# Modulation vectors in unbroken steps of three weight chunks, with GpSimd's queue for their loads and sums

## The chip, the cores and the metric

The kernel runs on one core of a Trainium2 chip. The metric is the device time of one execution in microseconds (us); lower is better. TensorE (PE) multiplies, VectorE (DVE) and ScalarE (ACT) do elementwise work, GpSimd (POOL) does some of it and issues DMAs, SyncE (SP) issues most DMAs. Each engine works through its own list of instructions in order and waits on semaphores for the others.

## The reference

A first block of two layers (attention beside a long convolution) is followed by a second one (a mixer, a dense feed-forward part, a state-space mixer, a mixture of experts). Each of the four parts of the second block has a modulation, computed from one vector `c`:

```python
def adaln(c, w, b):
    m = jax.nn.silu(c.astype(jnp.float32)) @ w + b
    shift, scale, gate = jnp.split(m, 3, axis=-1)
    return shift[:, None, :], scale[:, None, :], gate[:, None, :]
...
    sh, sc, g = adaln(c, e_mod_mix_w[j], e_mod_mix_b[j])
    h = rmsnorm(x, e_norm_mix[j]) * (1.0 + sc) + sh
```

`c` has 1024 elements and `w` is 1024 x 3072, float32, so each modulation is one row times 12.6 MB of weights: 50.3 MB for the four, each element used once.

## The kernel before

The four modulations don't depend on `x`, so the kernel computes them in the background of the first block. Python generators are registered as tasks with a rate. The projections of the first block call `tick` after each piece of work (some 57 times from the start of the first layer to the point named below), and a tick lets a task take as many steps (`yield` to `yield`) as its rate has added up to: 0.65 per tick for `modulations` (`ADALN_RATE` 65). A scheduler then puts all instructions into an order for each engine, so the order of the program isn't the order on the engine. Ahead of the last projection of the second layer `self.finish(self.adalns)` (L903) takes all steps that are left.

`modulations` waits `ADA_SKIP` = 8 steps and then runs `adaln` for four keys. The weights lie in memory as 24 chunks of 512 KB per modulation (128 partitions x 4 KB), one for each 128 outputs. A group is four chunks. Each chunk is loaded on SyncE's queue into one of three buffers `rawm` (`AR_BUFS`), and eight small matmuls (L947) multiply it: the 1024 inputs stand in eight columns of `silu`, and pairs of them land on four separate groups of 32 partitions of the PSUM tile `acc`, the 32 rows of a group all alike. After every second chunk there is a `yield` (`ADA_STEP` = 2), so that other work can come between. When four chunks are done, ScalarE copies `acc` to `ads` (L952), TensorE transposes it in four pieces (L955), and VectorE adds the four partial sums into `adv` (L956). After six groups come the bias and the norm's gain, one more transpose (L963), and the gate's row goes to memory on SyncE's queue (L966). These are 13 steps per modulation, 60 with the eight skipped.

The projections' weights take the same SyncE queue: `wchunk` loads 512 KB into one of a few `raw` buffers (L264), ScalarE rounds it to `whi` (L207), VectorE subtracts for `wlo` (L210), and three matmuls use them (L220 to L222, L322 to L324 where the weights are the left operand). At the end of a layer `x_done` computes the row statistics of x, TensorE transposes x with them (L439), and the first projection of the next part can begin. A load into a `rawm` buffer waits until the eight matmuls of the chunk that was in it are done, and whatever stands behind it on its queue waits too.

Of the kernel before, what the change touches and what calls it, by code (L numbers as in the profile page):

```python
# [14 lines left out]
AF = mybir.ActivationFunctionType  # L15
ALU = mybir.AluOpType
AX = mybir.AxisListType
# [3 lines left out]
P = 128  # L21
# [97 lines left out]
class Net:  # L119
    def __init__(self, ctx, tc, a, out):  # L120
        self.ctx, self.tc, self.nc, self.a, self.out = ctx, tc, tc.nc, a, out
        self.uid, self.ring, self.extra, self.left, self.hold, self.held = 0, {}, 0, 0, None, 0
        self.tasks = []
        self.dq = (tc.nc.gpsimd, tc.nc.sync, tc.nc.scalar)[DQ]
        self.gate, self.pool_lo = [], 0
        self.rows, self.cols = {}, {}
        e = ctx.enter_context
        self.cst = e(tc.tile_pool(name="cst", bufs=1))
        self.act = e(tc.tile_pool(name="act", bufs=1))
        self.mod = e(tc.tile_pool(name="mod", bufs=1))  # L130
        self.sm = e(tc.tile_pool(name="sm", bufs=8))
        self.ps = e(tc.tile_pool(name="ps", bufs=1, space=PSUM))
        self.dram = e(tc.tile_pool(name="dr", bufs=1, space=DRAM))
        self.wp = e(tc.tile_pool(name="wp", bufs=1, reuse_waits="tile"))
        self.raws, self.hls = [(self.wp, RAW_BUFS)], [(self.wp, HL_BUFS)]
# [770 lines left out]
    def first_block(self):  # L906
        pool = lambda name: self.tc.tile_pool(name=name, bufs=1, reuse_waits="tile")
        with pool("b1") as self.b1:
# [9 lines left out]
            for l in range(2):  # L918
                if l == 0:
                    self.adalns = self.task(self.modulations(), ADALN_RATE / 100)  # L920
                self.first_layer(l, H)
# [1 line left out]
            self.finish()  # L923


    def adaln(self, key, pool, raw_alloc):

        nc, a = self.nc, self.a  # L930
        V = nc.vector
        w = a[key + "_w"]
        cols = self.cols[key] = self.t(self.cst, [P, 2, 8], "col" + key)
        row = self.rows[key] = self.t(self.dram, [D], "row" + key)
        bc = self.load(self.sm, a[key + "_c"], [P, 4, 8], "adb", bufs=1, eng=self.dq)
        ad = self.t(self.sm, [P, 24], "adv", bufs=1)
        silu = self.silu_cols(pool)
        for m0 in range(0, 24, 4):
            acc = self.psB()
            for m in range(m0, m0 + 4):  # L940
                raw = raw_alloc()
                nc.sync.dma_start(raw, w[m])
                cs = slice((m - m0) * P, (m - m0 + 1) * P)
                for r in range(2):
                    for j in range(4):
                        k = 2 * j + r
                        nc.tensor.matmul(acc[32 * j:32 * j + 32, cs], silu[:, k:k + 1].broadcast_to([P, 32]),  # L947
                                         raw[:, k * P:(k + 1) * P], start=r == 0 and m == m0, stop=r == 1, skip_group_check=True)
                if m % ADA_STEP == ADA_STEP - 1 and m < m0 + 3:
                    yield  # L950
            s = self.t(pool, [P, 512], "ads", bufs=1)
            nc.scalar.activation(s, acc, AF.Copy)  # L952
            pt = self.psB()
            for i in range(4):
                nc.tensor.transpose(pt[:, i * P:(i + 1) * P], s[:, i * P:(i + 1) * P], self.ident)  # L955
            V.tensor_reduce(ad[:, m0:m0 + 4], pt.rearrange("p (m j r) -> p m j r", m=4, j=4)[:, :, :, 0], AX.X, ALU.add)  # L956
            yield
        V.tensor_tensor(cols[:, 1], ad[:, 0:8], bc[:, 0], ALU.add)
        V.scalar_tensor_tensor(cols[:, 0], ad[:, 8:16], 1.0, bc[:, 1], ALU.add, ALU.add)
        V.tensor_tensor(cols[:, 0], cols[:, 0], bc[:, 3], ALU.mult)  # L960
        V.tensor_tensor(bc[:, 2], ad[:, 16:24], bc[:, 2], ALU.add)
        pt = self.psB()
        nc.tensor.transpose(pt[0:8, 0:P], bc[:, 2], self.ident)  # L963
        r = self.t(self.act, [P, P], "dg", bufs=2)[0:8, :]
        nc.scalar.copy(r, pt[0:8, 0:P])
        self.dq.dma_start(row.rearrange("(m n) -> m n", n=P), r)  # L966
        yield

    def silu_cols(self, pool):
# [10 lines left out]
    def modulations(self):  # L980
        raw = lambda: self.t(self.b1, [P, D], "rawm", bufs=AR_BUFS)
        for _ in range(ADA_SKIP):
            yield
        for k in ("e_mod_mix", "e_mod_ffn", "o_mod_mix", "o_mod_ffn"):
            yield from self.adaln(k, self.b1, raw)
            if k == "e_mod_ffn":
                for _ in range(ADA_SKIP1):
                    yield

    def adaln_task(self, key, pool, rate):  # L990
        return self.task(self.adaln(key, pool, self.raw), rate)

    def gate_row(self, key):
        self.mgt = self.bcast(self.mod, self.rows[key], D, "mgt")
# [944 lines left out]
LATE1 = 0  # L1939
LATE2 = 0  # L1940
PRIO = 3000
ADALN_RATE = 65
S5_RATE = 70
RAW2_BUFS = 11
RAW3_BUFS = 5
# [98 lines left out]
AR_BUFS = 3  # L2044
# [12 lines left out]
MGV = 3  # L2057
HOLDP = 2
HOLDC = 0
ADA_STEP = 2  # L2060
ADA_SKIP = 8
ADA_SKIP1 = 0
```

## Time and profile before

| | us |
|---|---|
| median of 3 runs | 1993.03 (1983.26 to 1996.6) |
| profiled execution | 1992.76 |
| its span | 1991.0 |
| TensorE busy | 1869.4 (94%) |
| VectorE busy | 1555.7 (78%) |
| ScalarE busy | 1190.1 (60%) |
| GpSimd busy | 196.9 (10%) |

The first block ends near 570 us; the mixer begins near 641 us, the dense part near 800. Matmuls are pipelined and their ends are modelled, so busy time of TensorE is an upper figure. float32 matmuls leave two records each (L947: 768 matmuls, 1536 records).

### The profile page before, as it was taken

The numbers are of one execution on the slowest core, as the hardware profiler recorded it, in microseconds if no ns is written. First come the engines' busy times: TensorE is split into PE (matmuls) and PEld (weight loads), VectorE is DVE, ScalarE is ACT, GpSimd is POOL, SyncE is SP. The second block draws the span as 40 slices with busy tenths as digits, with TensorE's granted clock in tenths as the row PEclk, the third lists the DMA queues.
The fourth block names the chain that finished last, engine by engine and source line by source line (L and its number), as shares of the span: only waits on it lengthen the run. The fifth ranks groups of instructions, "written<-read, shape, count | busy, mean of one in ns | idle before, by whom it ended". The sixth has DMA issues, their size and how long they took to land.

```text
span 1991.0 us, 31217 instructions
## 1 busy us (share of the span) xinstructions
PE 1869.4 (94%) x11450; PEld 1580.4 (79%) x11450; DVE 1555.7 (78%) x2484; ACT 1190.1 (60%) x1628; POOL 196.9 (10%) x319
## 2 busy tenths in 40 slices
PE   7899989999976998889988989999999999999997
PEld 6787767887754977779978978888888888888875
DVE  6687577686432756788878678999999999999897
ACT  6564445554322843434445358787788877877775
POOL 0000000000010011872212210010001000100000
PEclk9999999999977987999999789999999999999999
DMA  8635656755687631557666568999999999999991
GB/s 259 193 121 171 209 177 210 253 161 191 221 280 237 174 102 51 173 210 234 216 238 251 216 238 282 374 323 377 352 369 316 379 353 378 324 382 357 356 346 57
DMA packets 254826, 503.37 MB, mean 253 GB/s; under 512 B 20082, under 2 KB 97396, under 8 KB 252616
## 3 DMA queue, kind: packets, MB, share of 16 engines
q1 hardware_dynamic: 253848, 498.47, 72.5%
q0 software_dynamic: 816, 2.82, 0.4%
q8 instruction: 92, 1.51, 0.3%
q14 instruction: 70, 0.57, 0.1%
HBM read 485.47 MB, written 15.75 MB: 252 GB/s over the span
## 4 chain that ended last, share of the span: by engine, by line
PE 77%; DVE 8%; DMA 6%; issue 3%; POOL 3%; ACT 3%; SPq 0%; ACTq 0%; DVEq 0%; POOLq 0%
PE A L220 12%; PE A L222 12%; PE A L221 12%; PE B L220 6%; PE B L221 6%; PE B L222 6%; PE A L322 3%; PE A L323 3%; PE A L324 3%; PE B L947 3%; DVE wlo L210 2%; DMA k<-in_flt_deltas_dram 1%; DMA rawm<-in_o_mod_ffn_w_dram 1%; PE B L1743 1%; PE B L439 1%
## 5 line engine op out<-in xcount | busy, mean ns | idle before, releaser
L210 DVE TENSOR_TENSOR wlo<-raw,whi 128x1024 fp32r<-128x1024 f32 x777 | 935.0, 1227 | 190.1 <-ACT whi L207 178.7
L207 ACT ACTIVATE whi<-raw 128x1024 fp32r<-128x1024 f32 x777 | 813.5, 1057 | 369.9 <-PE A L222 141.6
L221 PE MATMUL A<-wlo,hTh 128*128 128x512 f32 (+1 forms) x752 | 288.6, 384 | 1.6 <-DVE wlo L210 1.3
L220 PE MATMUL A<-whi,hTh 128*128 128x512 f32 (+1 forms) x752 | 285.4, 387 | 4.2 <-ACT hTh L207 4.2
L222 PE MATMUL A<-whi,hTl 128*128 128x512 f32 (+1 forms) x752 | 286.9, 383 | 0.9 <-DVE hTl L210 0.9
L322 PE MATMUL A<-hTh,whi 128*128 128x256 f32 x864 | 248.4, 288 | 7.7 <-ACT whi L207 4.3
L324 PE MATMUL A<-hTh,wlo 128*128 128x256 f32 x864 | 246.6, 285 | 1.4 <-DVE wlo L210 1.4
L323 PE MATMUL A<-hTl,whi 128*128 128x256 f32 x864 | 246.8, 286 | 1.0 <-DVE hTl L210 1.0
L322 PEld LDWEIGHTS A<-hTh,whi 128*128 128x128 f32 x864 | 167.1, 193 | 12.0 <-ACT whi L207 4.5
L323 PEld LDWEIGHTS A<-hTl,whi 128*128 128x128 f32 x864 | 167.3, 194 | 3.6 <-issue 1.4
L324 PEld LDWEIGHTS A<-hTh,wlo 128*128 128x128 f32 x864 | 167.2, 193 | 3.7 <-DVE wlo L210 1.8
L220 PEld LDWEIGHTS A<-whi,hTh 128*128 128x128 f32 x752 | 141.7, 189 | 35.4 <-ACT hTh L207 4.9
L221 PEld LDWEIGHTS A<-wlo,hTh 128*128 128x128 f32 x752 | 141.8, 189 | 33.3 <-DVE wlo L210 4.9
L222 PEld LDWEIGHTS A<-whi,hTl 128*128 128x128 f32 x752 | 142.0, 189 | 31.0 <-DVE hTl L210 2.0
L221 PE MATMUL A<-wlo,xg 128*128 128x512 f32 (+1 forms) x384 | 143.5, 374 | 0.0
L222 PE MATMUL A<-whi,xg 128*128 128x512 f32 (+1 forms) x384 | 143.0, 372 | 0.0
L220 PE MATMUL A<-whi,xg 128*128 128x512 f32 (+1 forms) x384 | 141.7, 376 | 0.0
L221 PE MATMUL B<-wlo,mhh 128*128 128x512 f32 x352 | 138.7, 394 | 0.0
L222 PE MATMUL B<-whi,mhl 128*128 128x512 f32 x352 | 137.6, 391 | 0.0
L220 PE MATMUL B<-whi,mhh 128*128 128x512 f32 x352 | 120.9, 394 | 0.2 <-ACT mhh L207 0.2
L947 PE MATMUL B<-rawm,silu 128*32 128x128 f32 x1536 | 70.8, 312 | 22.0 <-DMA rawm<-in_o_mod_ffn_w_dram 14.3
L947 PEld LDWEIGHTS B<-rawm,silu 128*32 128x32 f32 x1536 | 45.0, 122 | 47.8 <-DMA rawm<-in_o_mod_ffn_w_dram 20.6
(575 smaller groups left out, 2974.1 us busy)
## 6 DMA issues: line engine op xcount, KB each, us to landing
raw<-in_o_exp_up_dram SPq DMA_DIRECT2D x176, 512.0 KB, 5.8
raw<-in_o_exp_down_dram SPq DMA_DIRECT2D x176, 512.0 KB, 6.1
raw<-in_o_exp_gate_dram SPq DMA_DIRECT2D x174, 512.0 KB, 5.7
raw<-in_w_in_dram SPq DMA_DIRECT2D x96, 512.0 KB, 5.1
rawm<-in_e_mod_mix_w_dram SPq DMA_DIRECT2D x24, 512.0 KB, 3.7
rawm<-in_e_mod_ffn_w_dram SPq DMA_DIRECT2D x24, 512.0 KB, 6.6
rawm<-in_o_mod_mix_w_dram SPq DMA_DIRECT2D x24, 512.0 KB, 4.9
raw<-in_e_w_in_dram SPq DMA_DIRECT2D x24, 512.0 KB, 4.2
```

What stands on the lines that cost most here:

```text
L207: nc.scalar.activation(hi, src, AF.Copy)
L210: (nc.gpsimd if lo_eng == "pool" else nc.vector).tensor_tensor(lo, src, hi.bitcast(F32), ALU.subtract)
L220: nc.tensor.matmul(out, ah, bh, start=first, stop=False)
L221: nc.tensor.matmul(out, ah, bl, start=False, stop=False)
L222: nc.tensor.matmul(out, al, bh, start=False, stop=last)
L322: nc.tensor.matmul(o, wh[:, ms], xh[:, k, :], start=k == 0 and m == 0, stop=False, **kw)
L323: nc.tensor.matmul(o, wh[:, ms], xl[:, k, :], start=False, stop=False, **kw)
L324: nc.tensor.matmul(o, wl[:, ms], xh[:, k, :], start=False, stop=k == 7, **kw)
L439: nc.tensor.matmul(o, x[:, ks], dg, start=True, stop=True)
L947: nc.tensor.matmul(acc[32 * j:32 * j + 32, cs], silu[:, k:k + 1].broadcast_to([P, 32]), raw[:, k * P:(k + 1) * P], start=r == 0 and m == m ...
L1743: nc.tensor.transpose(ptr[:, i * P:(i + 1) * P], sg[:, i * P:(i + 1) * P], self.ident)
```

## The change

Each step of `adaln` now takes three chunks in one piece, with no `yield` inside and under a high priority (`self.first()`), so that the scheduler puts their 24 matmuls behind each other. The loads are issued from GpSimd's queue (`self.mq`), by `fetch`: the first three ahead of a modulation's first step, and those of the next step at the end of a step. Within a step the chunk that was loaded last is multiplied first. ScalarE copies 384 columns. The transposes and sums of each group are replaced: four small DMAs per step, also on GpSimd's queue, take one row of each of the four partition groups (3 x 512 bytes) to the tile `adp` of 96 rows, and at the end of a modulation one transpose of 96 rows and one sum over four give all 24 columns. The bias load and the gate's row use GpSimd's queue as well. A modulation has 10 steps (48 in all with the eight skipped), at a rate of 0.80 per tick. The loads of the projections' weights stay on SyncE's queue.

```diff
-    def adaln(self, key, pool, raw_alloc):
+    def adaln(self, key, pool, raw_alloc, bufs):
...
-        bc = self.load(self.sm, a[key + "_c"], [P, 4, 8], "adb", bufs=1, eng=self.dq)
+        bc = self.load(self.sm, a[key + "_c"], [P, 4, 8], "adb", bufs=1, eng=self.mq)
         ad = self.t(self.sm, [P, 24], "adv", bufs=1)
+        parts = self.t(self.sm, [96, P], "adp", bufs=1)
         silu = self.silu_cols(pool)
-        for m0 in range(0, 24, 4):
+
+        def fetch(m0):
+            raws = [raw_alloc() for _ in range(bufs)]
+            for i in range(bufs):
+                self.mq.dma_start(raws[i], w[m0 + i])
+            return raws
+
+        raws = fetch(0)
+        yield
+        for m0 in range(0, 24, bufs):
             acc = self.psB()
-            for m in range(m0, m0 + 4):
-                raw = raw_alloc()
-                nc.sync.dma_start(raw, w[m])
-                cs = slice((m - m0) * P, (m - m0 + 1) * P)
-                for r in range(2):
-                    for j in range(4):
-                        k = 2 * j + r
-                        nc.tensor.matmul(acc[32 * j:32 * j + 32, cs], silu[:, k:k + 1].broadcast_to([P, 32]),
-                                         raw[:, k * P:(k + 1) * P], start=r == 0 and m == m0, stop=r == 1, skip_group_check=True)
-                if m % ADA_STEP == ADA_STEP - 1 and m < m0 + 3:
-                    yield
-            s = self.t(pool, [P, 512], "ads", bufs=1)
-            nc.scalar.activation(s, acc, AF.Copy)
-            pt = self.psB()
-            for i in range(4):
-                nc.tensor.transpose(pt[:, i * P:(i + 1) * P], s[:, i * P:(i + 1) * P], self.ident)
-            V.tensor_reduce(ad[:, m0:m0 + 4], pt.rearrange("p (m j r) -> p m j r", m=4, j=4)[:, :, :, 0], AX.X, ALU.add)
+            with self.first():
+
+                for i in reversed(range(bufs)):
+                    cs = slice(i * P, (i + 1) * P)
...
+                s = self.t(pool, [P, bufs * P], "ads", bufs=1)
+                nc.scalar.activation(s, acc[:, :bufs * P], AF.Copy)
+            for j in range(4):
+                self.mq.dma_start(parts[24 * j + m0:24 * j + m0 + bufs], s[32 * j:32 * j + 1].rearrange("o (m p) -> o m p", m=bufs))
+            if m0 + bufs < 24:
+                raws = fetch(m0 + bufs)
             yield
+        pt = self.psB()
+        nc.tensor.transpose(pt[:, 0:96], parts, self.ident[0:96, 0:96])
+        V.tensor_reduce(ad, pt[:, 0:96].rearrange("p (j m) -> p m j", j=4), AX.X, ALU.add)
...
-        self.dq.dma_start(row.rearrange("(m n) -> m n", n=P), r)
+        self.mq.dma_start(row.rearrange("(m n) -> m n", n=P), r)
...
-            yield from self.adaln(k, self.b1, raw)
-            if k == "e_mod_ffn":
-                for _ in range(ADA_SKIP1):
-                    yield
+            yield from self.adaln(k, self.b1, raw, AR_BUFS)
...
-ADALN_RATE = 65
+ADALN_RATE = 80
```

On TensorE, at the end of the first block, the list of before holds the last matmuls of the output projection (`A<-whi,hTh`), then the modulations' chunks and transposes up to the transposed x (L439); of its 32 chunks behind the projection the first eight stand here:

```order
L222 MATMUL A_6249<-whi_6282,hTl_5598 128x512
L955 MATMUL B_5747<-ident_78,ads_5745 128x128 x4
L947 MATMUL B_5753<-rawm_5754,silu_1532 32x128 x8
L947 MATMUL B_5753<-rawm_5764,silu_1532 32x128 x8
L947 MATMUL B_5753<-rawm_5774,silu_1532 32x128 x8
L947 MATMUL B_5753<-rawm_5784,silu_1532 32x128 x8
L955 MATMUL B_5796<-ident_78,ads_5794 128x128 x4
L947 MATMUL B_5802<-rawm_5803,silu_1532 32x128 x8
L947 MATMUL B_5802<-rawm_5813,silu_1532 32x128 x8
L947 MATMUL B_5802<-rawm_5823,silu_1532 32x128 x8
L947 MATMUL B_5802<-rawm_5833,silu_1532 32x128 x8
L955 MATMUL B_5845<-ident_78,ads_5843 128x128 x4
```

In the changed kernel the same place (its lines are one to fourteen higher) holds:

```order
L223 MATMUL A_6273<-whi_6306,hTl_6083 128x512
L970 MATMUL B_6180<-ident_78,adp_5451 128x96
L977 MATMUL B_6187<-ident_78,adb_5448 8x128
L440 MATMUL B_6385<-dg_6383,x_75 128x128 x4
L440 MATMUL B_6397<-dg_6383,x_75 128x128 x4
L221 MATMUL A_6483<-whi_6487,hTh_6365 128x512
```

All 32 chunks have moved ahead of the projection's end, and the transposed x follows the projection directly. Ahead of it, a step of the changed kernel stands in TensorE's list as here, where the gap to the next step is the shortest of all (the second and third step of the first modulation):

```order
L959 MATMUL B_1582<-rawm_1440,silu_1264 32x128 x8
L959 MATMUL B_1582<-rawm_1439,silu_1264 32x128 x8
L959 MATMUL B_1582<-rawm_1438,silu_1264 32x128 x8
...
L221 MATMUL B_1689<-k_275_1315,fwdh_319 128x512
L222 MATMUL B_1689<-k_276_1316,fwdh_319 128x512
L223 MATMUL B_1689<-k_275_1315,fwdl_320 128x512
L221 MATMUL B_1690<-k_275_1315,fwdh_319 128x512
L222 MATMUL B_1690<-k_276_1316,fwdh_319 128x512
L223 MATMUL B_1690<-k_275_1315,fwdl_320 128x512
L959 MATMUL B_1776<-rawm_1615,silu_1264 32x128 x8
```

Three chunks follow each other, and between the two steps stand 14 matmuls of the first block (the eight left out are attention's). On GpSimd, the head of the changed list is:

```order
L201 DMA subln_277<-in_subln_dram 128x128
L195 DMA adb_1260<-in_e_mod_mix_c_dram 128x32
L945 DMA rawm_1270<-in_e_mod_mix_w_dram 128x1024
L945 DMA rawm_1271<-in_e_mod_mix_w_dram 128x1024
L945 DMA rawm_1272<-in_e_mod_mix_w_dram 128x1024
L201 DMA subln_3425<-in_subln_dram 128x128
L945 DMA rawm_1438<-in_e_mod_mix_w_dram 128x1024
L945 DMA rawm_1439<-in_e_mod_mix_w_dram 128x1024
L945 DMA rawm_1440<-in_e_mod_mix_w_dram 128x1024
L965 DMA adp_1263<-ads_1432 3x1x128 x4
```

Before, only the two loads of `subln` stood there; the first three chunks stood on SyncE's queue behind the first weights. The loads of the next step now come ahead of the four small DMAs of the step before them.

## Rows read from the trace of the kernel before

**Rows 1.** The page: busy time, TensorE's granted clock and GB/s in 40 slices.
```profile
PE 1869.4 (94%) x11450; PEld 1580.4 (79%) x11450; DVE 1555.7 (78%) x2484; ACT 1190.1 (60%) x1628; POOL 196.9 (10%) x319
PEclk9999999999977987999999789999999999999999
GB/s 259 193 121 171 209 177 210 253 161 191 221 280 237 174 102 51 173 210 234 216 238 251 216 238 282 374 323 377 352 369 316 379 353 378 324 382 357 356 346 57
```

**Rows 2.** By stretch: length, busy PE, PEld, DVE, ACT, POOL, clock, DMA, GB/s.
```profile
150.00:570.00 420.00, 405.15 (x3055) 329.68 (x3054) 287.54 (x560) 198.48 (x322) 0.00 (x0) 0.99 0.61 203
570.00:643.00 73.00, 44.97 (x585) 29.46 (x583) 14.66 (x58) 15.66 (x33) 6.07 (x8) 0.65 0.76 256
...
284.00:306.00 22.00, 13.91 (x78) 11.71 (x80) 18.50 (x53) 10.48 (x22) 0.00 (x0) 0.77 0.36 116
500.00:550.00 50.00, 47.91 (x369) 36.60 (x368) 24.27 (x30) 19.01 (x24) 0.00 (x0) 1.00 0.62 213
```

**Rows 3.** Chain of waits near 611 us, in order of time: start, us, what.
```profile
611.83 4.47 DMA rawm<-in_o_mod_ffn_w_dram
...
617.56 0.61 ACT ads L952
618.21 1.12 PE B L955 x4
```

**Rows 4.** TensorE's matmuls in order of time: start, us, what; idle time before it.
```profile
287.93 0.40 PE L221 MATMUL A<-wlo,hTh 128*128 128x512 f32 x1
288.17 0.39 PE L222 MATMUL A<-whi,hTl 128*128 128x512 f32 x1
294.74 3.75 PE L439 MATMUL B<-dg,x 128*128 128x128 f32 x16 [5.25 <-DVE sm L341]
301.13 0.50 PE L220 MATMUL A<-whi,hTh 128*128 128x512 f32 x1 [2.65 <-ACT hTh L207]
...
569.62 0.40 PE L222 MATMUL A<-whi,hTl 128*128 128x512 f32 x1
641.46 0.48 PE L220 MATMUL A<-whi,hTh 128*128 128x512 f32 x1
```

**Rows 5.** L947 in 570:643, L955 in 150:570, L947's group there, one run.
```profile
570.00:643.00 73.00, 29.55 (x512) 17.80 (x512) 0.65 0.76 256
...
150.00:570.00 420.00, 9.13 (x61) 7.46 (x62) 0.99 0.61 203
...
L947 PE MATMUL B<-rawm,silu 128*32 128x128 f32 x1024 | 41.2, 277 | 2.1 <-DMA rawm<-in_o_mod_mix_w_dram 2.1
...
560.75 1.52 PE L947 MATMUL B<-rawm,silu 128*32 128x128 f32 x48
```

**Rows 6.** Line L200 (loads on GpSimd, two on SP), then the tile rawm.
```profile
L200 POOL DMA_DIRECT2D subln<-in_subln_dram x2: 545/630/715, 1.3 to 51.4; - x2
L200 POOL DMA_DIRECT2D mgt<-rowe_mod_mix x1: 533/533/533, 572.1 to 572.1; - x1
DMA to landing us min/median/max: 3.6/5.5/6.6
...
DMA to landing us min/median/max: 3.5/4.5/6.9
```

**Rows 7.** Waits of SyncE's queue from 140 to 660 us; the weights' split.
```profile
SPq L942 <- PE B L947: 121.4, 62, 8.9
...
L210 DVE TENSOR_TENSOR wlo<-raw,whi 128x1024 fp32r<-128x1024 f32 x777 | 935.0, 1227 | 190.1 <-ACT whi L207 178.7 <-DMA raw<-in_o_exp_down_dram 1.4 <-DMA raw<-in_o_exp_up_dram 1.2
```

**Rows 8.** The first 18 us in order of time.
```profile
1.30 0.71 POOL L200 DMA_DIRECT2D subln<-in_subln_dram  x1 [0.36 <-issue]
7.30 0.23 DVE L840 TENSOR_SCALAR subln<-subln 128x128 f32<-128x128 f32 x1 [7.30 <-DMA subln<-in_subln_dram]
8.93 6.74 PE L439 MATMUL B<-dg,x 128*128 128x128 f32 x32 [8.93 <-DVE dg L420]
17.00 1.42 SPq L942 DMA_DIRECT2D rawm<-in_e_mod_mix_w_dram  x3
```

More of the change, by code (lines that the diff above doesn't have):

```diff
@@ L123, in __init__ @@
         self.tasks = []
+        self.mq = tc.nc.gpsimd
         self.dq = (tc.nc.gpsimd, tc.nc.sync, tc.nc.scalar)[DQ]
@@ new lines, in fetch @@
+        def fetch(m0):
[6 more added lines that the diff above has]
+        for m0 in range(0, 24, bufs):
+            acc = self.psB()
+            with self.first():
+                for i in reversed(range(bufs)):
+                    cs = slice(i * P, (i + 1) * P)
+                    for r in range(2):
+                        for j in range(4):
+                            k = 2 * j + r
+                            nc.tensor.matmul(acc[32 * j:32 * j + 32, cs], silu[:, k:k + 1].broadcast_to([P, 32]),
+                                             raws[i][:, k * P:(k + 1) * P], start=r == 0 and i == bufs - 1, stop=r == 1,
+                                             skip_group_check=True)
+                s = self.t(pool, [P, bufs * P], "ads", bufs=1)
+                nc.scalar.activation(s, acc[:, :bufs * P], AF.Copy)
+            for j in range(4):
+                self.mq.dma_start(parts[24 * j + m0:24 * j + m0 + bufs], s[32 * j:32 * j + 1].rearrange("o (m p) -> o m p", m=bufs))
+            if m0 + bufs < 24:
+                raws = fetch(m0 + bufs)
@@ L984, in modulations @@
         for k in ("e_mod_mix", "e_mod_ffn", "o_mod_mix", "o_mod_ffn"):
-            yield from self.adaln(k, self.b1, raw)
-            if k == "e_mod_ffn":
-                for _ in range(ADA_SKIP1):
-                    yield
+            yield from self.adaln(k, self.b1, raw, AR_BUFS)
     def adaln_task(self, key, pool, rate):
-        return self.task(self.adaln(key, pool, self.raw), rate)
+        return self.task(self.adaln(key, pool, self.raw, 2), rate)
     def gate_row(self, key):
@@ L2059 @@
 HOLDC = 0
-ADA_STEP = 2
 ADA_SKIP = 8
-ADA_SKIP1 = 0
```

## Prediction

> **What bounds the kernel now.** Read the page first: TensorE is busy for 94% of the span, and of the slices in which its granted clock stands at 7 tenths, two lie side by side, from about 547 to 647 us [rows 1]. A kernel like this gains where TensorE waits or runs at the lower clock, so the second view is the table by stretch. From 150 to 570 us TensorE is busy for 405.15 of 420 us at a clock of 0.99. From 570 to 643 us it is busy for 44.97 of 73 us at 0.65 [rows 2]. The chain of waits shows what that second stretch holds: nothing but the rest of the modulations. A pair of weight chunks is multiplied, the next pair is waited for (4.47 us here), ScalarE copies the group (0.61), four transposes follow (1.12), and it starts again [rows 3]. I call it the tail. In order of time, the last matmul of the first block's output projection starts at 569.62 us and the first of the mixer at 641.46 [rows 4]. Of the 96 chunks, 64 (1024 records) are multiplied before 570 us and 32 (512 records) in the tail [rows 5].
>
> **What the change does, and its terms.** All are taken against the profiled execution (1992.76 us; the median of the runs shown is 1993.03, so a difference carries over).
>
> *The tail.* Before, 60 steps run at 0.65 per tick; now 48 at 0.80. Some 57 ticks lie between the start of the first layer and the point where the rest is drained: 37 steps before, 45 now, so three remain instead of 23. The order agrees: 23 matmuls of the projection follow the last step, and behind those come two transposes, not 32 chunks. What stays there is the change of layer itself: statistics, transposed input, split. The same change of layer earlier in the trace takes from 288.17 to 301.13 us, 12.96 us, with TensorE waiting 5.25 and 2.65 [rows 4]. So 641.46 - 569.62 - 12.96 = 58.9 us go.
>
> *Matmuls and transposes.* All 96 chunks are now multiplied ahead of the tail. Three in one run took 1.52 us [rows 5], so 32 steps take 48.6. They take the place of 41.2 us for 64 chunks in scattered runs and 9.13 us of transposes [rows 5]; four transposes of each kind remain, about 1.0 us. Sum: 48.6 + 1.0 - 41.2 - 9.1 = -0.7. The wait for a chunk ahead of the tail, 2.1 us [rows 5], is taken into the next term: -2.1.
>
> *The fetch.* This decides. A step reads all three buffers, and the next three loads (1.57 MB) can be issued only when its matmuls are done, because there are three buffers and no fourth. Between two steps TensorE has other matmuls: (405.15 - 41.2 - 9.13) / 31 = 11.4 us on average [rows 2, 5], but unevenly. Counted in the order and priced with the trace's matmuls (0.23 to 0.24 us for 512 columns [rows 4]), the shortest two gaps are 4.0 and 5.7 us, seven are below 9, fourteen at 10 or less, 23 at 12 or less. If a fetch takes F, the shortfalls of the 31 gaps add up to 3 us at F = 6.4, 7 at 8, 19 at 9.7, 40 at 11, 62 at 12, 85 at 13, 130 at 14.8. No row has three such loads on GpSimd's queue, so F is bounded. Below: the quickest landing of the line that loads on that queue, 3.6 us [rows 6] (two of its nine loads are SyncE's), and two more loads at the page's highest rate, 382 GB/s [rows 1], 1.4 each: 6.4. Above: the slowest of them, 6.6, and two loads at half of the tail's 256 GB/s [rows 2], 4.1 each: 14.8. I take the median landing, 5.5, and two loads at the full 256 GB/s, 2.1 each: F = 9.7, 19.4 us. The middle is nearest because the weights alone will ask for some 125 GB/s in this stretch: 203 GB/s over 420 us are 85 MB, of which 33.5 are the 64 chunks. Issuing costs 0.53 to 0.71 us of GpSimd each [rows 6], a second and a third behind the first; that engine has nothing else to do there, and its landings include it.
>
> The first matmul of a step waits for the third load. Behind it stands all of TensorE's work, behind ScalarE's copy of the group (queued early) the splits of the weights, and behind those VectorE's. All three lose the same time once, not thrice.
>
> *SyncE's queue.* 96 loads leave it, with 121.4 us in which it waited for rawm buffers while the weights stood behind [rows 7]. I cost this at nothing: TensorE lost only 14.85 us in 420 [rows 2], most of it at the change of layer.
>
> *GpSimd's queue.* Its other entries in the stretch: the second bias load and the store of the gate row wait for ScalarE's copy at the end of each modulation, and the next fetch stands behind them. Two issues and that wait are 2 to 3 us; the gaps there are about average, so 1 each for three of them: 3. The 128 small transfers to `adp` (four per step, 2.2 us of issues) stand behind the fetch and delay nothing, except at the very end. There ScalarE's copy, four issues and a landing (0.6 + 2.2 + 3.6 to 6.6) meet a cover of about 5.3 us: 1 to 4 us too long, partly beside the statistics of the change of layer. I take 1.
>
> *The start.* The first three loads are not behind the first weights any more (17.00 us) but right behind the load of subln (1.30 us), which VectorE awaits until 7.30 [rows 8]. Wholly in the way, 1.57 MB at 256 GB/s are 6 us; wholly hidden, 0. TensorE starts on x at 8.93 us [rows 8] and by then the loads share with x and the first weights: 2.
>
> *VectorE, ScalarE, clock.* Twenty small sums fewer on VectorE, and as many columns copied by ScalarE as before (32 times 384 for 24 times 512), leave the path as it is; both engines are idle for a third to a half of this stretch [rows 2]. The granted clock was 0.77 around the change of layer, with waits of 5.25 and 2.65 us, but 1.00 from 500 to 550 us with one of 2.1 [rows 2, 4, 5]. Short waits for fetches should cost little clock: 2 (0 to 8).
>
> Sum: -58.9 - 0.7 - 2.1 + 19.4 + 3 + 1 + 2 + 2 = -34.3, so 1992.8 - 34.3 = 1958.5 us.
>
> **The rivals.** *Short fetches.* The queue is free and each load is whole rows of 4 KB; at F = 6.4 the sum is 16 us lower: 1942. For it speaks the landing of 3.6 us; against it, that the pairs of before landed in up to 6.9 us beside the weights [rows 6]. The Trainium skill, DMA: Bandwidth & Descriptors, section on the anatomy of a DMA on the gpsimd path, has a fit of 2.0 us plus bytes over 436 GB/s for one transfer; for 1.57 MB that is an estimate of 5.6 us, by which the time would be about 1941. No row here shows such a load without others beside it.
>
> *Long fetches, and no gain.* One set of three buffers means that nothing is in flight while a step is multiplied, and a fetch that outlasts its gap stops TensorE. At F = 11.7 the shortfalls are 55 us and all that the tail gave is paid back: 1994. This needs each of the two later loads to take 3.1 us (170 GB/s). For it speaks that weights and chunks together are then 102 MB in some 440 us, 232 GB/s on average where the stretch had 203, and more in the short gaps; against it, that the tail moved 256 and other slices over 350 [rows 1, 2].
>
> *Longer still: slower.* From F = 12.5 (73 us) on the kernel is slower by 1%; at F = 13, 2024, and at the upper bound, 2069.
>
> *Descriptors held up by VectorE.* If each issue had to wait for one VectorE instruction of the split (1227 ns on average [rows 7]), F grows by 3.7 to 13.4, 95 us: 2034. Against it: the seven issues of that line on GpSimd took 533 to 715 ns whatever VectorE did [rows 6], while it is busy for 68% of this stretch [rows 2]. The Trainium skill, SBUF — State Buffer, section SBUF: two separate sides, speaks against the change here: VectorE's two-port modes lock GpSimd out of a shared port, so that DMAs issued there appear blocked. By that rule the time would be the 2034 of this rival; the trace does not agree so far, and no row has a long series of such issues.
>
> That the tail stays is excluded by the order, apart from the three steps named.
>
> **How the numbers follow.** Forecast (F from 8 to 11, 1946 to 1979): 0.42. Short: 0.20. Long without gain (1980 to 2013): 0.20. Longer: 0.13. VectorE: 0.05. A measurement of this kernel can tell about 1% from no change (1973 to 2013). Nearly all of the first two are faster: 0.62; the third and the edges same: 0.22; slower 0.16. The range leaves out the lower edge of the short case and the two slow ones: 1940 to 2010. The forecast's own range is 1946 to 1979.
>
> **What would show it.** Right: the mixer's first matmul some 34 us earlier, about 13 us behind the last of the projection; TensorE's waits for rawm spread over some fourteen of 31 steps, 1 to 3 us each, 5 to 6 at the shortest gap. Wrong: waits at nearly every step (long fetch), GpSimd issues far over 0.7 us (VectorE), weights late at VectorE's or ScalarE's splits (bandwidth), a first L221 after 18 us (start).

## The result and the profile after

The changed kernel takes 1929.36 us (median of 4 runs, 1927.88 to 1931.11) beside 1991.3 us for the kernel before on the same chip: a ratio of 0.9691, 95% interval 0.966 to 0.9721. In a second set of six runs it took 1927.07 us, ratio 0.968 (0.9649 to 0.971). It is faster by 3%, and 10.6 us below the lower end of the range, 1940. The profiled execution has a span of 1928.3 us, 62.7 below that of before.

The page's busy line, clock and traffic, as in [rows 1]:

```profile
PE 1829.9 (95%) x11358; PEld 1561.2 (81%) x11358; DVE 1548.4 (80%) x2464; ACT 1191.9 (62%) x1636; POOL 323.6 (17%) x551
PEclk9999999999989979989987989999999999999998
GB/s 259 205 166 213 233 258 241 278 237 192 278 213 171 119 42 178 197 229 217 212 267 160 307 219 363 351 343 359 370 352 335 363 365 363 342 375 358 342 352 24
```

The two slices at 7 tenths side by side are gone. TensorE at the boundary of the first block, in order of time (start, us, what, idle time before), answers to [rows 4]:

```profile
559.04 0.40 PE L223 MATMUL A<-whi,hTl 128*128 128x512 f32 x1
560.05 0.27 PE L970 MATMUL B<-ident,adp 96*128 96x96 f32 x1 [0.61 <-DMA adp<-ads]
561.19 0.27 PE L977 MATMUL B<-ident,adb 128*8 128x128 f32 x1 [0.87 <-DVE sm L333]
562.91 3.64 PE L440 MATMUL B<-dg,x 128*128 128x128 f32 x16 [1.45 <-DVE sm L342]
569.23 0.51 PE L221 MATMUL A<-whi,hTh 128*128 128x512 f32 x1 [2.69 <-ACT whi L208]
```

Behind the last matmul of the projection stand two transposes and the change of layer, and the mixer starts at 569.23 us, where it was 641.46. Busy time by stretch (length, then busy PE, PEld, DVE, ACT, POOL, clock, DMA share, GB/s), first the kernel before, then the changed one, from the start to the end of that last matmul and from there to the mixer:

```profile
0.00:570.02 570.02, 536.88 (x3876) 442.83 (x3877) 396.84 (x779) 289.06 (x469) 1.67 (x7) 0.98 0.61 200
570.02:641.46 71.44, 44.23 (x583) 29.17 (x582) 13.12 (x52) 14.10 (x29) 6.07 (x8) 0.64 0.76 255
```

```profile
0.00:559.44 559.44, 532.61 (x4330) 445.61 (x4330) 396.28 (x770) 295.94 (x485) 120.88 (x238) 0.99 0.71 234
559.44:569.23 9.79, 4.18 (x18) 3.69 (x18) 7.00 (x34) 5.96 (x17) 6.61 (x9) 0.83 0.23 62
```

So the 62.7 us are: 570.02 - 559.44 = 10.6 ahead of the boundary, 71.44 - 9.79 = 61.6 at it, and 9.6 are lost behind it (1928.3 - 569.2 against 1991.0 - 641.5). The surprise is the first number. The forecast had it at 21.6 us longer, not 10.6 shorter.

Of the 9.6 us, 4.5 lie in the first few us of the mixer, since the mark doesn't cut the two kernels at the same work. Before, all 32 transposes of x stand ahead of the mixer's first matmul:

```profile
636.27 5.43 PE L439 MATMUL B<-dg,x 128*128 128x128 f32 x32
...
644.08 0.39 PE L220 MATMUL A<-whi,hTh 128*128 128x512 f32 x1
```

Now 16 of them stand behind its first thirteen matmuls, which run at a lower clock:

```profile
575.37 0.63 PE L221 MATMUL A<-whi,hTh 128*128 128x512 f32 x1
575.80 2.30 PE L440 MATMUL B<-dg,x 128*128 128x128 f32 x16
```

From the mixer's first matmul to its thirteenth are 6.1 us where it was 4.0, at a granted clock of 0.54 (569.23 to 575.80 us) where it was 1.00: 2.1 us. The 16 transposes bring 2.3 more, which the 61.6 contain and which are only moved.

The fetch, which was to decide, can be seen in the view of the tile rawm (issues on GpSimd with their shortest, median and longest ns; who waited for it; landings in us):

```profile
L945 POOL DMA_DIRECT2D rawm<-in_e_mod_mix_w_dram x24: 527/537/560, 2.5 to 205.8; - x24
...
  PE B L959: 5.0, 5
...
DMA to landing us min/median/max: 3.6/6.0/9.5
```

TensorE waited for chunks five times, 5.0 us in all. From the first issue of a fetch to the third landing the 31 fetches took 6.5 to 10.6 us, 8.3 on average: the first landing after 4.9, the other two 3.4 later.

### The profile page after: what moved, and what is told of

Same layout as the page of the kernel before. It is cut to its first block, busy times and chain, and to the rows that moved or that the text cites. A ratio compares the mean times of both kernels' runs of the same rounds, so it can differ in the third digit from the quotient of the medians.

```text
span 1928.3 us, 31270 instructions
## 1 busy us (share of the span) xinstructions
PE 1829.9 (95%) x11358; PEld 1561.2 (81%) x11358; DVE 1548.4 (80%) x2464; ACT 1191.9 (62%) x1636; POOL 323.6 (17%) x551
## 4 chain that ended last, share of the span: by engine, by line
PE 73%; issue 11%; DVE 6%; POOL 5%; DMA 4%; ACT 2%; SPq 0%; POOLq 0%; ACTq 0%; DVEq 0%
PE A L223 12%; PE A L222 12%; PE A L221 12%; PE B L221 6%; PE B L222 5%; PE B L223 5%; PE A L323 3%; PE A L325 3%; PE A L324 3%; PE B L959 2%; DMA rawm<-in_e_mod_mix_w_dram 2%; DVE wlo L211 1%; PE B L1754 1%; PE B L1732 1%; PE B L1101 1%
## 5 line engine op out<-in xcount | busy, mean ns | idle before, releaser
L222 PEld LDWEIGHTS A<-wlo,xg 128*128 128x128 f32 x384 | 72.4, 189 | 12.9 <-DVE wlo L211 0.3
L223 PEld LDWEIGHTS A<-whi,xg 128*128 128x128 f32 x384 | 72.3, 188 | 12.6
```

What stands on the lines that cost most here:

```text
L222: nc.tensor.matmul(out, ah, bl, start=False, stop=False)
L223: nc.tensor.matmul(out, al, bh, start=False, stop=last)
```

## The experiments

"Boundary" is the end of the first block's last projection matmul, "other waits" are TensorE's idle time ahead of it without its waits for chunks (before: 33.1 - 2.1 = 31.0 us; changed: 26.8 - 5.0 = 21.9, and 22.0 in the second profile). "Half clock" is time at a granted clock of 0.5, the lower of TensorE's two levels. Ratios are to the kernel before on the same chip.

**What the rate alone does.** The kernel before with one number changed:

```diff
-ADALN_RATE = 65
+ADALN_RATE = 100
```

> The kernel before with one number changed, the rate of the modulations' steps (0.65 to 1.00 per tick), so that all 96 chunks come ahead of the boundary in its own order; pairs and single chunks, SyncE's queue and the transposes stay. Theory A: the tail goes here too (about 58 to 62 us), and 32 more transposes (4 to 5 us) stay on TensorE: 1932 to 1942 us. Theory B: more loads that wait in front of the weights on SyncE's queue give back 10 to 40 us: 1943 to 1975 us.

1949.06 us, ratio 0.9806 (0.9786 to 0.9827). The tail is gone (9.84 us from boundary to mixer), but the boundary stands at 585.89, 26.5 us behind the changed kernel's. Busy time of the chunks' matmuls and of the group transposes up to the boundary, in this kernel:

```profile
0.00:585.89 585.89, 57.89 (x1536) 39.84 (x1536) 0.99 0.68 222
...
0.00:585.89 585.89, 14.71 (x96) 11.44 (x96) 0.99 0.68 222
```

In the changed kernel the same views give

```profile
0.00:559.44 559.44, 48.72 (x1536) 40.24 (x1536) 0.99 0.71 234
...
0.00:559.44 559.44, 0.74 (x3) 0.42 (x3) 0.99 0.71 234
```

21.4 of the 26.5 us are TensorE's busy time (554.0 us ahead of the boundary where the changed kernel has 532.6), the other 5.0 idle time. The views give 9.2 of it to the chunks in smaller runs and 14.0 to the transposes. These are upper figures, since a run's last matmul is counted beyond the start of the next matmul; counted from start to start they are 7 and 10, and 4.5 more lie in TensorE's other matmuls. Waits for chunks were 3.9 us, other waits 28.0. Theory A had named the transposes, at 4 to 5 us, and not the runs. By the ratios the rate alone gives about two thirds of the gain; most of the rest is the form of the step.

**The rate taken back** (`ADALN_RATE = 80` to `65` in the changed kernel).

> The changed kernel with the old rate of steps (0.65 per tick): 75 chunks come ahead of the boundary and 21, seven steps, behind it. Theory A: seven fetches in a row with nothing beside them, each 6.5 to 8 us (the landings of the changed kernel's third loads took 6.5 to 10.6 us beside other work) and a step at half the clock of about 3 us, less some 10 us of matmuls and stalls that are then missing ahead of the boundary: 1929 + 56 to 77 - 10 = 1975 to 1996 us. Rival (the step's new form carries the gain, not the rate): under 1960 us.

1983.88 us, ratio 0.998 (0.996 to 1.000). 21 chunks come back behind the boundary, and from there to the mixer are 72.1 us. TensorE, in order of time:

```profile
566.26 2.79 PE L959 MATMUL B<-rawm,silu 128*32 128x128 f32 x48 [7.15 <-DMA rawm<-in_o_mod_ffn_w_dram]
575.88 2.79 PE L959 MATMUL B<-rawm,silu 128*32 128x128 f32 x48 [6.83 <-DMA rawm<-in_o_mod_ffn_w_dram]
```

A fetch with next to nothing beside it (1.25 of the 9.55 MB from 565 to 612 us are not chunks or their sums) costs 5.6 to 7.2 us of waiting, and a step takes 2.79 us at half clock (granted clock 0.53 from 565 to 625 us), as the theory had it. From first issue to third landing these fetches took 6.9 to 8.1 us. The fit of the Trainium skill, DMA: Bandwidth & Descriptors, section on the anatomy of a DMA on the gpsimd path, is for one transfer; the prediction's estimate from it, 5.6 us for the bytes of all three loads, is under what the trace has even here.

**Transposes put back** into the changed kernel, nothing else:

```diff
-            for j in range(4):
-                self.mq.dma_start(parts[24 * j + m0:24 * j + m0 + bufs], s[32 * j:32 * j + 1].rearrange("o (m p) -> o m p", m=bufs))
+            pt = self.psB()
+            for i in range(bufs):
+                nc.tensor.transpose(pt[:, i * P:(i + 1) * P], s[:, i * P:(i + 1) * P], self.ident)
+            V.tensor_reduce(ad[:, m0:m0 + bufs], pt[:, :bufs * P].rearrange("p (m j r) -> p m j r", m=bufs, j=4)[:, :, :, 0], AX.X, ALU.add)
```

(The tile `adp` and the last transpose and sum of each modulation, which read it, are taken out too.)

> The changed kernel with the group sums as before: three transposes on TensorE and a sum on VectorE per step, no transfers to adp. Theory A (part of the gain is TensorE's own work: the kernel before with the rate 1.00 spent 11.6 us on 96 transposes and 53.4 us on the chunks ahead of the boundary, the changed one 0.6 and 46.8): 92 more transposes are 9 to 12 us and the last transfers' wait at the boundary (0.6 us) goes: 1937 to 1941 us. Rival (the transfers in GpSimd's queue cost as much as the transposes did): 1926 to 1932 us.

1939.04 us, ratio 0.9715 (0.9693 to 0.9738). That is 10 to 12 us above the two medians of the changed kernel, as theory A said, and 5 to 7 by the ratios, whose intervals overlap. In the trace the boundary stands at 570.58, 11.1 us later: 12.3 us more busy time, less 1.2 of idle time. Waits for chunks fell from 5.0 to 0.6 us, as the transposes make the gaps longer (the shortest two are 6.0 and 7.3 us in this trace, 4.8 and 5.9 in the changed kernel's); the other waits rose by 3.2. So the transposes' price is seen, and the 128 small transfers show none in the changed kernel apart from 0.61 us at the boundary.

**The loads' queue.** Two runs of the changed kernel and one of the kernel before, with the line that issues a load changed (to `nc.sync` in the first, shown here, to `nc.scalar` in the second, and from `nc.sync` to `nc.gpsimd` in the kernel before):

```diff
-                self.mq.dma_start(raws[i], w[m0 + i])
+                nc.sync.dma_start(raws[i], w[m0 + i])
```

> The changed kernel with its chunk loads back on SyncE's queue; the bias load, the sums' transfers and the row store stay on GpSimd's. Theory A (the gain is the tail, and rate and step length took it away): no chunk is multiplied behind the boundary here either, so 1925 to 1936 us whichever queue loads. Theory B (taking the loads off SyncE's queue is worth something of its own: before the boundary TensorE was idle for 33.1 us before and 26.8 after, and most of the waits that went were for data that SyncE's queue loads): weights stand behind chunk loads that wait for a buffer until a step is multiplied, so 1937 to 1960 us, with SyncE waiting for the modulation's matmuls for over 100 us.

> The changed kernel with its chunk loads issued by ScalarE, so off SyncE's queue and off GpSimd's too. Theory A (GpSimd's queue is worth its 11 us over SyncE's only because nothing waits behind it): ScalarE's own splits wait behind a load that waits for a step's matmuls, which costs 5 to 25 us, and the final drain of GpSimd shrinks from 9.8 to 2 us, which gives back some 3: 1931 to 1950 us. Rival (any queue that is not SyncE's does as well, and the drain is all that GpSimd adds): 1923 to 1928 us.

> The kernel before with the chunk loads alone on GpSimd's queue; rate, pairs, transposes and tail stay. Theory A: the tail stays as long, and GpSimd's final drain grows by some 4 us for 96 more issues (0.72 us with 8 issues before, 9.78 with 240 after): 1990 to 1999 us. Theory B: the waits ahead of the boundary shrink by some 8 us: 1978 to 1988 us.

With all loads on SyncE's queue: 1938.37 us, ratio 0.9755 (0.9734 to 0.9776); other waits 28.0, boundary 570.43. The chain of waits shows one place (start, us, what):

```profile
272.61 7.94 DMA k<-in_flt_deltas_dram
280.55 0.02 issue
280.57 0.63 ACT k L575
...
282.51 1.33 ACT k L582 x2
283.85 0.95 ACT whi L208
```

and what TensorE lost by it:

```profile
284.85 0.80 PE L221 MATMUL A<-whi,hTh 128*128 128x512 f32 x1 [4.12 <-ACT whi L208]
```

A load of the filter's constants (256 KB) lands 7.94 us after its issue, with three chunk loads issued right behind it on the same queue. ScalarE waits for it, and behind that wait stands a split of weights. The changed kernel has no such wait there. That the chunk loads made it late is not shown: in the run with rate 0.65, with all chunk loads on GpSimd's queue, such a load takes 8.44 us at 327 us. On ScalarE's queue the loads cost other waits of 26.6 us and save GpSimd's drain: 1930.39 us, ratio 0.9657 (0.962 to 0.9694), the same as the changed kernel within the noise. In the kernel before, moving the loads to GpSimd and nothing else gives 2000.0 us, ratio 1.0063 (1.004 to 1.0086): theory A's sign, but more than its drain. The tail took 81.5 us instead of 71.4 and the end some 2 more; ahead of the boundary nothing changed (569.7). So the queue alone is worth nothing in the kernel before; why the tail grew by 10 us there is not shown.

**Which loads?** The same line again, with SyncE for the first fetch alone (`key == "e_mod_mix" and m0 == 0`), and for all but the first:

> The changed kernel with only its first fetch, three loads of 96, back on SyncE's queue; the other 93 stay on GpSimd's. TensorE's rows are then in the order of the kernel before in the stretch from about 75 to 125 us (22 of 360 places differ, against 191 in the changed kernel), and in the order of the changed kernel from the sixth step on. Theory O (a good part of the unforeseen gain comes from the order in which the work around 100 us stands, which hangs on where the first fetch is issued): waits of 3 to 4 us near 97 us and of 1 to 2 near 120 us and the half clock behind them return, 1934 to 1941 us. Theory Q (the queue of the loads makes the difference of 9 us to the run with all loads on SyncE's): 1927 to 1932 us.

> The mirror image: the first fetch on GpSimd's queue, the other 93 loads on SyncE's. TensorE's rows stand as in the changed kernel from row 400 to 900 of its other work. Theory O: the waits near 97 and 120 us stay away, and GpSimd's final drain is short: 1925 to 1931 us. Theory Q: weights behind 93 loads that wait for buffers, 1936 to 1942 us.

1935.17 us (ratio 0.972, 0.9689 to 0.9751) and 1932.44 us (0.9698, 0.9665 to 0.9731). Other waits 28.2 and 28.6: each half loses the whole 6 us, in its own places. The first brings back waits of before that go with the order of the matmuls there. In the kernel before

```profile
96.47 0.50 PE L578 MATMUL B<-k,fT 128*128 128x512 f32 x1 [3.87 <-ACT Hr L612]
120.34 0.50 PE L221 MATMUL B<-kf,fwdh 128*128 128x512 f32 x1 [1.50 <-DVE kf L210]
122.74 0.98 PE L220 MATMUL B<-kf,fwdh 128*128 128x512 f32 x3 [1.24 <-ACT kf L207]
```

where the changed kernel has only

```profile
121.76 0.96 PE L221 MATMUL B<-kf,fwdh 128*128 128x512 f32 x3 [0.71 <-ACT kf L208]
```

and with only the first fetch on SyncE's queue

```profile
93.59 0.51 PE L579 MATMUL B<-k,fT 128*128 128x512 f32 x1 [2.62 <-ACT Hr L613]
```

The other runs bear this out. Of TensorE's matmuls, chunks and their transposes left out, the 441st to the 700th (84 to 134 us before, 85 to 120 in the changed kernel) stand in the order of before in four other runs (loads on SyncE's queue, first fetch on it, half of the bytes, and the kernel before a tick earlier); these and the kernel before wait 3.4 to 6.6 us from 90 to 127 us. Eight other runs have the changed kernel's order there, and with it wait 0.4 to 1.9 us. The run with all but the first fetch on SyncE's queue is one of these eight. It loses 2.79 us at 285 us, behind the load named above (6.61 us here), and the rest in smaller waits. With the first fetch alone on SyncE's queue a load of these constants takes 6.5 us too at that place, and TensorE waits 1.23. Theory O is right for its place, and neither theory for the sum; the time of the second run, with a spread of 1926 to 1940 us, hardly differs from the changed kernel's.

**The fetch.** Half of the bytes (the second half of each chunk is not loaded and the first is multiplied twice, so the modulations are not the reference's), two chunks per step with two buffers and a rate of 1.17, and a step in the order of its loads (`for i in range(bufs)` for `reversed(range(bufs))`):

> The changed kernel with half of each chunk loaded (128 rows of 2 KB for 4 KB), and the matmuls reading that half twice, so that the work on TensorE is the same and the modulations are not the reference's. Theory A (bytes make the length of a fetch, 8.3 us from the first issue to the third landing in the changed kernel, and TensorE's waits for chunks, 5.0 us, are what is left over in the short gaps): third landings after 5.5 to 6.5 us, waits under 2 us, 1923 to 1927 us, and GpSimd's final drain of 9.8 us as it is, since there are as many rows. Rival (a fixed price for each load or row sets it): landings and time as in the changed kernel, 1927 to 1931 us.

> The changed kernel with two buffers and steps of two chunks, 48 steps at 1.17 per tick instead of 32 at 0.80. The gaps between steps, counted in this kernel's order and priced as the prediction did, are 6 us or less 11 times, 7 us or less 17 times of 47. In the changed kernel the second landing came 4.9 to 8.9 us (mean 6.5) after a fetch's first issue, some 0.4 us of which lie beside the step itself. Theory A (a fetch that outlasts its gap stops TensorE by the difference): at 6.1 us the shortfalls add up to 25 us where they are 5.0, so 1945 to 1955 us. Rival (the gaps hide fetches whatever the count says): 1927 to 1935 us.

> The changed kernel with the three chunks of a step multiplied in the order in which they are loaded, not in reverse: the first matmuls of a step wait for the first landing and not for the third (on average 2.6 us earlier), and where the scheduler sees a gap it puts other work between chunks (52 runs of chunks instead of 32; TensorE's other rows stand as in the changed kernel up to about 125 us). If the waits for the third landing are what is left over (5.0 us in one profile, 5.2 in the other): under 3 us of waits for chunks and 1922 to 1927 us. Rival (a step in pieces releases its buffers later, so that the next fetch comes later and the waits move to it): 1927 to 1935 us.

Half of the bytes: fetches of 4.6 to 8.2 us (6.1 on average) and no wait for a chunk at all, as theory A said, but 1943.17 us, ratio 0.9748 (0.9719 to 0.9777). The shorter loads also changed the scheduler's order, near 100 us to that of the kernel before: other waits 29.9, with 3.88 us at 98.6. The expected time is missed by this: 8 us more of other waits, and 8.5 more busy time with 27.3 us at half clock. In order of the loads: waits for chunks 1.5 us, and 1936.76 us, ratio 0.973 (0.9708 to 0.9751), other waits 26.6: again the waits went and the time did not. Here the steps fell into 52 runs of chunks, whose busy time rose from 48.7 to 53.0 us.

Steps of two: 1994.54 us, ratio 1.0015 (0.9989 to 1.004), where 1945 to 1955 was expected. The waits for chunks were 29.3 us, close to the 25 counted. The rest was missed. Two of the waits:

```profile
274.73 1.93 PE L959 MATMUL B<-rawm,silu 128*32 128x128 f32 x32 [7.33 <-DMA rawm<-in_e_mod_ffn_w_dram]
282.02 1.30 PE L959 MATMUL B<-rawm,silu 128*32 128x128 f32 x20 [4.32 <-DMA rawm<-in_e_mod_ffn_w_dram]
```

The stretch to the boundary:

```profile
0.00:622.37 622.37, 553.67 (x4332) 456.25 (x4332) 399.83 (x775) 299.48 (x502) 154.86 (x303) 0.95 0.64 210
```

63 us longer: 42 of idle time (24 for chunks, 10 for the last transfers to adp at the end of three modulations, the rest spread) and 21 of busy time, at a mean clock of 0.95 where it was 0.99. TensorE stood at half clock for 58.0 us where it was 10.2: with waits of 3 to 7 us the clock goes, and the work behind them is slower too.

**Luck of the order, or the change?** The changed kernel again, in three other orders of the same instructions, and the kernel before in one (`ADALN_RATE` 84 and 79, `ADA_SKIP` 7):

> The changed kernel once more, unchanged, for what belongs to it and what to one execution. If the waits and the half clock ahead of the boundary belong to the kernel: last projection matmul ended at 557 to 562 us, 25 to 29 us of idle TensorE and 10 to 14 us of half clock before it (559.4, 26.8 and 10.2 in its first profile). If they belong to the execution: 565 to 571 us and 17 to 30 us of half clock, as in the runs with loads on SyncE's or ScalarE's queue.

> The changed kernel with steps at 0.84 per tick instead of 0.80: the same instructions, in another order (708 of 1782 places of TensorE's other work differ ahead of the boundary), all 96 chunks still ahead of it. Theory L (of the 12 to 14 us that TensorE's other work takes less ahead of the boundary, a good part is the luck of one order, as the runs with three loads moved or with a step's order turned round, 1935 and 1937 us, suggest): 1930 to 1940 us. Rival (it belongs to the change, whatever the exact order): 1925 to 1930 us.

> The changed kernel with the first step one tick earlier (7 ticks skipped instead of 8), all else as it is: the same instructions in another order again. Theory L: 1930 to 1940 us. Rival: 1925 to 1930 us.

> The changed kernel with steps at 0.79 per tick: the order is the changed kernel's up to about 125 us and differs behind it, all 96 chunks ahead of the boundary. Theory L: 1930 to 1940 us, and if the waits near 100 us alone made the luck, at the lower end. Rival: 1925 to 1930 us.

> The kernel before with its first step one tick earlier: the same instructions in another order, the tail as long less at most one step (about 4 us). Theory L (orders scatter by some 5 us either way, and the kernel before may stand on the bad side): 1978 to 1988 us. Rival: 1986 to 1993 us.

Again: boundary 562.35, 27.7 us idle, and 17.1 us of half clock, where 10 to 14 were expected. The other orders: 1938.65 (0.9758, 0.9728 to 0.9788), 1938.64 (0.9754, 0.9725 to 0.9782) and 1937.26 us (0.9735, 0.9708 to 0.9762), and before 1992.14 us (1.0004, 0.9984 to 1.0024). By the times theory L would be right. The traces say otherwise: other waits are 21.8, 21.9 and 27.2 us, in two of three what they are in the changed kernel. Each of the three waits for 6 to 9 us at one place, here at rate 0.84:

```profile
529.47 1.52 PE L959 MATMUL B<-rawm,silu 128*32 128x128 f32 x48
540.16 2.79 PE L959 MATMUL B<-rawm,silu 128*32 128x128 f32 x48 [9.17 <-DMA rawm<-in_o_mod_ffn_w_dram]
```

Two steps stand in a row in TensorE's order, with no other matmul between them, and a whole fetch is waited for. With 7 ticks skipped it is the same (8.71 us). At rate 0.79 twelve matmuls stand between the two steps (3 us, and a wait of 6.14), and 2.81 us for the transfers to `adp` come on top. In the changed kernel no two steps stand so close; its shortest gap was counted at 4.0 us and is 4.8 in the trace. So the part that is luck is a gap of zero, worth some 9 us, and the changed kernel's time is the best of the four orders that were run.

## Why the prediction was wrong, step by step

- **The tail: right.** -58.9 forecast, -61.6 measured, of which 2.3 are the 16 transposes that only moved behind the mixer's start. The change of layer took 9.8 us and not 12.96: TensorE waited 1.45 and 2.69 us in it where [rows 4] had 5.25 and 2.65.
- **Matmuls and transposes: right.** -0.7 forecast. Busy time in 0 to the boundary: chunks 41.2 to 48.72, transposes 9.13 to 0.74 [rows 5]: -0.9. (Counted from start to start it is 2.8, and TensorE's other matmuls fall by 7.1 and not by the 3.3 below; the sum of the two is the same.)
- **The fetch: the mechanism held, the size did not.** 19.4 forecast, 5.0 measured. F was 8.3 on average and not 9.7, 0.5 of it beside the step's own matmuls. At 7.8 the prediction's own table gives some 6. The term was mis-sized in both of its parts: the first landing took 4.9 us and not 5.5, and the two later loads 1.7 each and not 2.1. The middle bound was taken for the weights' traffic (125 GB/s); with 234 GB/s in all the loads still came faster. And the table is steep there: 1.4 us of F, and 0.5 that overlapped, were 14 us of time. The zero gap shows the other side of it.
- **GpSimd's queue (3): not seen.** No fetch behind a row store was late; gaps there were longer than a fetch. The last transfers (1): 0.61 us.
- **The start (2): right.** TensorE starts on x at 7.87 and not 8.93 us (7.83 in the second execution), but that is lost again at once, by waits of 0.61 and 0.70 us at 15 and 17 us among others. Its 440th matmul, the same one in both kernels, starts at 85.3 us where it was 83.8, and at 86.3 in the second execution.
- **SyncE's queue at nothing: the step that took the time out of the range.** With the fetch at its measured 5.0 us the sum would have been 1944, inside it. The argument for nothing was that TensorE lost only 14.85 us in 420 [rows 2], a table that begins at 150 us. From the start to the boundary, other waits were 31.0 us and fell to 21.9, in a second execution to 22.0, and TensorE's other busy time fell from 486.5 to 483.2 (the busy time of the stretch without chunks and transposes), with less of the stretch at half clock (20.5 us before, 10.2 after, 17.1 in the second execution). No term of the sum was there for it. The runs show it as a property of the change in this form: two other orders have it, and moving either the first three loads or the other 93 back loses 6 us. Most of the 9 us has a place: 5.9 are the waits from 96 to 123 us, ahead of that table, which go with an order that the place of the first fetch decides (in all but the run with half of the bytes). Two waits of 1.7 us at 260 and 2.25 at 374 are gone, and a new one of 1.5 stands at 153 us. Why these last went, and why each half of the loads loses all, stays open; that constants come late behind chunk loads on SyncE's queue fits one place in two runs and is not shown as the cause.
- **Clock (2), behind the boundary.** From the mixer's start to the last store 1348.7 us after 1343.2, and 1347.6 in the second execution: 5.5 us. 2.1 of them are the lower clock in the mixer's first thirteen matmuls, so this term held, and 2.3 the 16 transposes that moved. For these the sum had no term: the change of layer that it took from [rows 4] has 16 transposes in it, the tail of before had 32. The last 1 us is not explained; all kernels run here lie between 1337 and 1350.
- **The end: not in the sum.** From the start of the last out_dram<-xg store to the end of the span 10.4 us after 6.3; see below.

Together: -10.6 - 61.6 + 5.5 + 4.0 = -62.7. Of the rivals the short fetch (1942 us) came nearest, for a reason it did not have. VectorE held up no issue: all 96 loads issued in 527 to 560 ns while VectorE was busy for 396 of 559 us. The rule of the Trainium skill, SBUF — State Buffer, section SBUF: two separate sides, did nothing here that a row shows; it is for VectorE's two-port modes, and whether the split ran in one no row says. The range failed because its low end was the shortest fetch with all else as forecast; no case let the rest of the stretch gain.

## What to carry to other kernels

Count the gaps, and look first for a gap of zero: one place in which two steps stand in a row costs more than thirty gaps that are a little short. Moving loads off a shared in-order queue can also change the order in which a scheduler puts other engines' work, so look at the waits of the whole stretch, its first part too, and let the range hold a gain there. When work moves off TensorE's path, its form (runs of matmuls, number of transposes) is worth measuring apart from its place: here the rate alone gave some 39 us, and the form of the step with its queue some 23 more.

## What the runs showed of the hardware

GpSimd's last instructions grew. The final drain of its queue (shortest, median and longest ns of three), in the kernel before, the changed one, and with the loads on SyncE's queue:

```profile
L2030 POOLq DRAIN  x3: 40/107/719, 1981.6 to 1990.7; - x3
```

```profile
L2041 POOLq DRAIN  x3: 46/107/9782, 1917.4 to 1928.1; - x3
```

```profile
L2041 POOLq DRAIN  x3: 107/179/1942, 1923.1 to 1934.1; - x3
```

It takes 9.78 us where GpSimd issued the 96 loads and the 128 small transfers, 9.21 with the loads alone of these (8.56 in the kernel before with its loads on GpSimd), 1.94 with the transfers alone, 0.72 with 8 issues. In the changed kernel it ends at 1927.20 us, after SyncE's last wait (1924.83), and the span ends behind both. From the last store to the end of the span nine profiles with loads and transfers on GpSimd in steps of three have 10.1 to 10.4 us, the three with neither 6.3 to 6.4, those with the loads alone 9.4 and 8.5, and those with the transfers alone 6.8 to 9.0. So the 4.0 us go with DMAs on GpSimd's queue, issued some 1,400 us earlier, but the drain is not all of it. In the changed kernel it ends 2.4 us behind SyncE's last wait. Another 1.3 us lie in SyncE's own waits, which end 6.8 us after the start of the last store and not 5.5. With the transfers alone and the loads on SyncE's queue the drain is over before the last store starts, and the end is still at 9.0; what holds SyncE there is not shown. With steps of two the same 96 loads left a drain of 5.13 us and an end of 8.0: by what law it grows is not shown.

The second thing is the price of the clock. In the run with rate 0.65 a step of three chunks takes 2.79 us behind the boundary, at a granted clock of 0.53, where it takes 1.52 between other work, and with steps of two 42 us more of waiting came with 21 us more of busy time, at 58.0 us of half clock instead of 10.2.

The third is how steep a single-buffered fetch is: 6.5 to 10.6 us, spread over 31 gaps, cost 5.0 us of waiting, and one gap of zero costs 8.7 to 9.2 by itself.
